# The six tiles for the weights' halves at six distances from a multiple of 512 bytes

## The chip, the cores and the metric

The kernel runs on one core of a Trainium2 chip. The metric is the device time of one execution in microseconds (us). The engines are named as in the profile: PE (TensorE matmul), PEld (its weight loads), DVE (VectorE), ACT (ScalarE), POOL (GpSimd), SP (SyncE, which issues DMAs).

## The reference

One layer of a diffusion transformer over 256 latent and 256 context tokens of width 2048, all in float32, batch 1, one layer deep. Cut to its core:

```python
mod = silu(c) @ w_mod + b_mod                      # six rows of 2048: sa, ca, ga, sm, cm, gm
h   = rmsnorm(x, w) * (1 + ca) + sa                # latent tokens; the context likewise with c_ctx
p   = h @ w_in                                     # q, k, v, pool input, two gates
a   = softmax(q1 k1) - lam * softmax(q2 k2)        # 8 heads, keys of latent and context
mix = (sig(g_a) * (rmsnorm(a v) @ w_a) + sig(g_b) * (pool(p) @ w_b)) @ w_o
x   = x + ga * mix
x   = x + gm * (relu(h2 @ w_ff1) ** 2 @ w_ff2)     # h2 = modulate(x), w_ff1 is 2048 x 8192
```

## The kernel before

Every weight is read from memory once, in chunks of 128 partitions x 1024 float32 (512 KB; the four `pool_w` chunks have 512). `load_next` brings a chunk into one of five `raw` tiles by a DMA on SP's queue and splits it: ACT rounds it to the matmul's reduced float32 (`act.copy(hi, raw)`, line 213) into a tile `whi`, and DVE subtracts (`vec.tensor_sub(lo, raw, hi)`, line 214) to get the rest, `wlo`. Activations are split into such pairs as well. A product is then three matmuls: high by high, low activation by high weight, high activation by low weight (`mm3`, lines 241 to 243; `xstat`, lines 410, 411 and 413; `ff1`, lines 939 and 942).

The order of the chunks is written out in a list by `plan`; `wchunk` hands out the next one and keeps two more loaded ahead. There are three `whi` and three `wlo` tiles (`bufs=3`). A new chunk takes any of the three whose last reader is done. Only the eight chunks of the first half of `w_k` go elsewhere, to a 16 KB tile `first` that holds four halves.

The tiles lie in SBUF in the order in which the code first asks for them, each row of a tile whole. So the three `whi` and three `wlo` tiles, each with a row of 4096 bytes, are neighbours. The ring of seven 16 KB tiles (`xT`, `cT`, `hL`, `hC`, `first`, later `act`, `mix` and others) lies ahead of them, and so do the nine 2 KB work tiles, the small ones, and the five `raw` tiles.

The work goes through stages. First the modulation stage: a loop over m = 1 to 7 multiplies chunks of `w_m` (`mod_chunk`, line 347), eight in a pass, into a row for four column blocks; `mod_rows` (line 352) copies it out, `mod_columns` turns it on PE, and `hidden` builds `hL` and `hC`, the modulated latent and context tokens. In the same loop `first_steps` works off, in steps of three matmuls, the first halves of `w_k` (latent `kx`, context `kc`) and `w_q`. The dictionary `carried` says after which chunk of a pass these begin, and after each `w_m` chunk one or two steps are taken:

```python
    for m in range(4, 8):
        carried[m] = ((0, "kc", m - 2), (2, "kx", m - 1), (4, "q", m - 1))
...
            gens += [first_steps(n, j) for at, n, j in carried[m] if at == i]
            todo = chain(*gens)
            steps(todo, 16 if i == 7 else 2 if i < 4 or m == 3 else 1)
```

So in a pass the `w_q` chunk comes after the fifth `w_m` chunk, and its four steps are taken one by one after the fifth, sixth, seventh and eighth. Then follow the rest of q, k and v, with the attention beside them, pooling, gates, `w_o`, and the feed-forward part in eight blocks (`ff1`, `ff2`). In these, chunks are used up one after the other.

The order of the instructions on each engine is not that of the code: a scheduler takes, for each engine, the earliest instruction in the code whose operands and tiles are ready by its own model of time, except where `tc.keep_in_program_order` (`pin`) holds an order. The order is then fixed in the program.

Of the kernel before, what the change touches and what calls it, by code (L numbers as in the profile page):

```python
# [11 lines left out]
F32 = mybir.dt.float32  # L12
F32R = mybir.dt.float32r
# [4 lines left out]
P = 128  # L18
# [30 lines left out]
def layer(ctx: ExitStack, tc, a, out):  # L49
    nc = tc.nc  # L50
    pool = ctx.enter_context(tc.tile_pool(name="sb", bufs=1))
# [23 lines left out]
    def s16(name, shape, dt=F32):  # L75
        return pool.tile(shape, dt, tag="s16", name=name, bufs=7)
# [34 lines left out]
    def raw_chunk(src, n=1024):  # L111
        raw = pool.tile([P, n], F32, tag="raw", name="raw", bufs=5)
        nc.sync.dma_start(raw, src)
        return raw
# [66 lines left out]
    def x1_tile():  # L181
        if not x1s:
            x1s.append(s16("x1", [P, 2, D]))
        return x1s[0]

    loaded = []
    done = [0]

    def load_next():
        key, rate = stream[len(loaded)]  # L190
        src = a[key[0]]
        for i in key[1:]:
            src = src[i]
        if key[0] == "prq":
            nc.sync.dma_start(prq, src)
            loaded.append((key, None, None))
            return
        if key[0] in ("cT", "x"):
            dst = cT[:, 4 * key[1]:4 * key[1] + 4, :] if key[0] == "cT" else x1_tile()[:, key[1], key[2] * 512:key[2] * 512 + 512]
            nc.sync.dma_start(dst, src)  # L200
            loaded.append((key, None, None))
            return
        n = src.shape[-1]
        raw = raw_chunk(src, n)
        if key[:2] == ("w_k", 0):
            if not first:
                first.append(s16("first", [P, 4, 1024], F32R))
            i = 2 * (key[2] % 2)
            hi, lo = first[0][:, i, :], first[0][:, i + 1, :]
        else:  # L210
            hi = pool.tile([P, n], F32R, tag="whi", name="whi", bufs=3)
            lo = pool.tile([P, n], F32R, tag="wlo", name="wlo", bufs=3)
        act.copy(hi, raw)  # L213
        vec.tensor_sub(lo, raw, hi.bitcast(F32))  # L214
        loaded.append((key, hi, lo))
        credit[0] += rate
        credit_rate[0] = rate
        while credit[0] >= 1.0:
            credit[0] -= 1.0
            if late[0] is not None:  # L220
                next(late[0], None)

    def wchunk(*key, ahead=AHEAD):
        while len(loaded) < min(done[0] + 1 + ahead, len(stream)) or loaded[done[0]][1] is None:
            if loaded and done[0] < len(loaded) and loaded[done[0]][1] is None:
                done[0] += 1
                continue
            load_next()
        got, hi, lo = loaded[done[0]]
        assert got == key, (got, key)  # L230
        loaded[done[0]] = None
        done[0] += 1
        tick()
        return hi, lo
# [857 lines left out]
```

## Time and profile before

| | |
|---|---|
| median of the runs shown | 1521.57 us (2 runs, 1521.33 to 1521.80) |
| the profiled execution | 1519.78 us, of which 1517.7 are the span from first to last instruction |
| granted TensorE clock | 0.994 |
| PE, DVE, ACT busy | 98%, 70%, 50% of the span |
| read from memory | 344.44 MB, 228 GB/s over the span |

In the profile a group of instructions is given by its line in the code, its engine and operation, the tiles written and read (without buffer numbers), shape and count. Behind the bar stand the group's busy time, the mean duration of one in ns, and the idle time of the engine ahead of them with what ended it. In the timeline the first column is the start in us, the second the duration (of a row with a count over 1: of them all). Durations of matmuls are those of a pipeline, and overlap: the distance of two starts is the pitch.

### The profile page before, as it was taken

What the parts mean: (1) busy time and instruction counts of PE and PEld (TensorE: products, weight loads), DVE (VectorE), ACT (ScalarE), POOL (GpSimd) and SP (SyncE); (2) the same over time, 40 slices, a digit from 0 to 9 for tenths busy, and PEclk for the clock granted to TensorE, in tenths of its full rate; (3) what the DMA queues carried; (4) which work ended last, traced back from release to release, by engine and by line L of the source; (5) the groups of instructions that cost most, each with busy time, mean ns of one, the idle gap of its engine ahead of it and who ended that gap; (6) DMA issues with size and microseconds to landing.
All of it is one profiled execution on the core that took longest, in us unless ns stands there. A gap on an engine that the chain in (4) does not pass through costs nothing.

```text
span 1517.7 us, 19767 instructions
## 1 busy us (share of the span) xinstructions
PE 1480.7 (98%) x7336; PEld 1232.8 (81%) x7336; DVE 1063.2 (70%) x1280; ACT 755.7 (50%) x1007; POOL 129.3 (9%) x124
## 2 busy tenths in 40 slices
PE   7899999999989999999999999999999999999998
PEld 5677877768878888888879988888888888888887
DVE  7799878777887767666757665666666555555675
ACT  6677534556655444444444554544444454444432
POOL 0100111000140000000000100100000000000170
PEclk9899999999999999999999999999999999999999
DMA  8888668556568787788755677767777666666664
GB/s 314 310 283 308 214 215 285 177 167 193 167 216 300 254 275 272 242 295 296 235 181 168 220 251 245 232 217 244 231 241 240 202 188 193 193 187 193 184 200 142
DMA packets 97439, 347.82 MB, mean 229 GB/s; under 512 B 11072, under 2 KB 11712, under 8 KB 97344
## 3 DMA queue, kind: packets, MB, share of 16 engines
q1 hardware_dynamic: 96768, 345.49, 70.4%
q8 instruction: 57, 0.93, 0.3%
q0 software_dynamic: 576, 1.08, 0.2%
q14 instruction: 38, 0.31, 0.1%
HBM read 344.44 MB, written 2.10 MB: 228 GB/s over the span
## 4 chain that ended last, share of the span: by engine, by line
PE 88%; issue 3%; DVE 3%; DMA 3%; ACT 1%; POOL 1%; DVEq 0%; SPq 0%; ACTq 0%; POOLq 0%
PE f L939 14%; PE f L411 8%; PE f L410 8%; PE f L413 8%; PE f L942 7%; PE pg L413 4%; PE pg L410 4%; PE pg L411 4%; PE pyy L410 2%; PE wo L410 2%; PE wo L413 2%; PE wo L411 2%; PE pyy L413 2%; PE pyy L411 2%; PE v L411 2%
## 5 line engine op out<-in xcount | busy, mean ns | idle before, releaser
L214 DVE TENSOR_TENSOR wlo<-raw,whi 128x1024 fp32r<-128x1024 f32 x507 | 628.6, 1244 | 365.2 <-ACT whi L213 350.9
L213 ACT CAST whi<-raw 128x1024 fp32r<-128x1024 f32 x507 | 529.8, 1047 | 587.3 <-PE f L411 178.1
L939 PE MATMUL f<-h,whi 128*128 128x512 f32 x896 | 224.2, 392 | 0.0
L411 PE MATMUL f<-whi,act 128*128 128x512 f32 x512 | 199.3, 389 | 0.0
L410 PE MATMUL f<-whi,act 128*128 128x512 f32 x512 | 199.3, 389 | 0.0
L939 PEld LDWEIGHTS f<-h,whi 128*128 128x128 f32 x896 | 161.5, 189 | 29.1
L588 DVE SCALAR_TENSOR_TENSOR macc<-raw,sil,macc 128x1024 f32<-128x1024 f32 x128 | 166.2, 1299 | 1.4 <-DMA raw<-in_w_cm_dram 0.8
L413 PE MATMUL f<-wlo,act 128*128 128x512 f32 x512 | 136.8, 389 | 0.0
L942 PEld LDWEIGHTS f<-h,wlo 128*128 128x128 f32 x896 | 122.2, 190 | 8.7
L942 PE MATMUL f<-h,wlo 128*128 128x256 f32 x896 | 124.9, 282 | 0.0
L413 PEld LDWEIGHTS f<-wlo,act 128*128 128x128 f32 x512 | 96.1, 188 | 20.0
L411 PEld LDWEIGHTS f<-whi,act 128*128 128x128 f32 x512 | 96.1, 188 | 19.8
L410 PEld LDWEIGHTS f<-whi,act 128*128 128x128 f32 x512 | 96.1, 188 | 19.8
L410 PE MATMUL pg<-whi,hL 128*128 128x512 f32 x256 | 100.5, 393 | 0.0
L411 PE MATMUL pg<-whi,hL 128*128 128x512 f32 x256 | 99.7, 389 | 0.0
L950 POOL TENSOR_TENSOR rsq<-relu 128x512 f32<-128x512 f32 x28 | 29.2, 1042 | 537.6 <-ACT relu L949 516.7
L413 PE MATMUL pg<-wlo,hL 128*128 128x512 f32 x256 | 68.6, 390 | 2.5 <-DVE wlo L214 2.5
L413 PEld LDWEIGHTS pg<-wlo,hL 128*128 128x128 f32 x256 | 48.0, 188 | 12.9 <-DVE wlo L214 2.9
L410 PEld LDWEIGHTS pg<-whi,hL 128*128 128x128 f32 x256 | 48.1, 188 | 10.1 <-issue 0.2
L411 PEld LDWEIGHTS pg<-whi,hL 128*128 128x128 f32 x256 | 48.1, 188 | 10.1 <-issue 0.2
L410 PE MATMUL wo<-whi,mix 128*128 128x512 f32 x128 | 49.9, 390 | 0.0
L411 PE MATMUL wo<-whi,mix 128*128 128x512 f32 x128 | 49.8, 389 | 0.0
(267 smaller groups left out, 2205.1 us busy)
## 6 DMA issues: line engine op xcount, KB each, us to landing
raw<-in_w_ff_dram SPq DMA_DIRECT2D x240, 512.0 KB, 4.3
raw<-in_w_m_dram SPq DMA_DIRECT2D x64, 512.0 KB, 4.9
raw<-in_w_ga_dram SPq DMA_DIRECT2D x32, 512.0 KB, 4.6
raw<-in_w_cm_dram SPq DMA_DIRECT2D x32, 512.0 KB, 4.6
raw<-in_w_gb_in_dram SPq DMA_DIRECT2D x32, 512.0 KB, 4.5
raw<-in_w_ga_in_dram SPq DMA_DIRECT2D x32, 512.0 KB, 4.4
raw<-in_w_sm_dram SPq DMA_DIRECT2D x32, 512.0 KB, 4.7
raw<-in_w_o_dram SPq DMA_DIRECT2D x32, 512.0 KB, 4.6
```

Of the source, the lines that this page charges most:

```text
L213: act.copy(hi, raw)
L214: vec.tensor_sub(lo, raw, hi.bitcast(F32))
L410: pe.matmul(banks[t], tok(h, k, 0, tt), wt, start=k == 0, stop=False)
L411: pe.matmul(banks[t], tok(h, k, 1, tt), wt, start=False, stop=False)
L413: pe.matmul(banks[t], tok(h, k, 0, tt), wt, start=False, stop=k == 2 * nk - 1)
L588: pin(vec.scalar_tensor_tensor(acc, raw, sil[:, 0, k:k + 1], acc, ALU.mult, ALU.add))
L939: pe.matmul(ps, hi[:, kk * P:kk * P + P], both(h2, k), start=k == 0, stop=False)
L942: pe.matmul(ps[:, T:2 * T], lo[:, kk * P:kk * P + P], act_slice(h2, k, 0), start=False, stop=k == KT - 1)
L950: gp.tensor_mul(sq, r, r)
```

## The change

The six tiles get names of their own, `whia` to `wloc`, each alone under its tag, and behind each a tile of 16 floats (64 bytes) is asked for that nothing uses. `half_tiles` makes them all at the first call; chunk number n then takes the pair n modulo 3.

```diff
+    halves = []
+    used = [0]
+
+    def half_tiles(n):
+
+        if not halves:
+            for part in ("whi", "wlo"):
+                for i in range(3):
+                    halves.append(pool.tile([P, 1024], F32R, tag=f"{part}{'abc'[i]}", name=f"{part}{'abc'[i]}", bufs=1))
+                    pool.tile([P, 16], F32, tag=f"gap{part}{'abc'[i]}", name="gap", bufs=1)
+        i = used[0] % 3
+        used[0] += 1
+        if used[0] <= 3:
+            return halves[i][:, 0:n], halves[3 + i][:, 0:n]
+        return [pool.tile([P, n], F32R, tag=f"{part}{'abc'[i]}", name=f"{part}{'abc'[i]}", bufs=1) for part in ("whi", "wlo")]
+
...
-            hi = pool.tile([P, n], F32R, tag="whi", name="whi", bufs=3)
-            lo = pool.tile([P, n], F32R, tag="wlo", name="wlo", bufs=3)
+            hi, lo = half_tiles(n)
```

## The prediction

> **What bounds the kernel now.** I read the page's busy shares and chain first, then the table by stage, then the costliest groups.
>
> ```profile
> PE 1480.7 (98%) x7336; PEld 1232.8 (81%) x7336; DVE 1063.2 (70%) x1280; ACT 755.7 (50%) x1007; POOL 129.3 (9%) x124
> PE 88%; issue 3%; DVE 3%; DMA 3%; ACT 1%; POOL 1%; DVEq 0%; SPq 0%; ACTq 0%; POOLq 0%
> 0.00:40.00 40.00, 28.36 (x132) 21.17 (x133) 28.62 (x45) 27.06 (x37) 1.82 (x6) 1.00 0.90 319
> 40.00:80.00 40.00, 35.72 (x135) 25.34 (x134) 32.99 (x48) 29.12 (x43) 7.23 (x4) 0.87 0.82 287
> 60.00:160.00 100.00, 97.45 (x428) 75.80 (x427) 90.45 (x149) 71.87 (x95) 0.00 (x0) 1.00 0.86 297
> 500.00:600.00 100.00, 100.00 (x450) 82.91 (x449) 70.75 (x68) 44.16 (x48) 1.48 (x2) 1.00 0.78 261
> 1000.00:1200.00 200.00, 200.00 (x1002) 170.19 (x1001) 130.31 (x135) 92.33 (x110) 8.34 (x8) 1.00 0.74 231
> ```
>
> The table's columns are the stretch, then busy time of PE, PEld, DVE, ACT and POOL, the granted clock, DMA share and GB/s. The reader is to see two regimes. From about 60 us on PE has no room: 97.45 of 100 us in the modulation stage, 100 of 100 later, at clock 1.00. In the first 60 us PE waits for weights: DMA share 0.90 in the first row, its highest. So the change can help only by shortening matmuls, and can hurt only where it leaves PE without work. DVE and ACT, which write the six tiles, have slack except in the modulation stage (90.45 and 71.87 of 100).
>
> **Part 1: the addresses.** Before, the six tiles are neighbours of 4096 bytes each, so all start at one distance from a multiple of 512. After, a 64-byte gap follows each: six distances. No instruction, byte or DMA is added by it, and `raw` is requested earlier and stays where it is. Do operands at one distance slow each other? The trace holds an experiment: for the first-half `w_k` chunks the halves go into `first`, in the ring of 16 KB tiles in which `hL` lies too. Adding up the code's row lengths from that ring to `whi` (single-value rows taken as 32 bytes) puts `whi` 256 bytes from it modulo 512. So these rows compare an output at `raw`'s distance with one 256 bytes off, and a matmul whose two operands lie at one distance with one whose operands lie 256 apart:
>
> ```profile
> L213 ACT CAST whi<-raw x507: 615/1053/1092, 11.5 to 1504.2; 128x1024 fp32r<-128x1024 f32 x168, 128x512 fp32r<-128x512 f32 x1
> L213 ACT CAST first<-raw x8: 1031/1053/1056, 27.1 to 153.4; 128x1024 fp32r<-128x1024 f32 x8
> L214 DVE TENSOR_TENSOR wlo<-raw,whi x507: 683/1225/2310, 12.5 to 1505.5; 128x1024 fp32r<-128x1024 f32 x168, 128x512 fp32r<-128x512 f32 x1
> L214 DVE TENSOR_TENSOR first<-raw,first x8: 1209/1225/1227, 28.8 to 154.5; 128x1024 fp32r<-128x1024 f32 x8
> L242 PE MATMUL w_k<-first,hL x32: 387/389/497, 30.1 to 165.1; 128*128 128x512 f32 x32
> L242 PE MATMUL w_q<-wlo,hL x32: 389/389/499, 36.2 to 167.8; 128*128 128x512 f32 x32
> ```
>
> The medians are equal to the nanosecond: 1053 and 1053, 1225 and 1225, 389 and 389. Steps of 64 bytes were not seen, so I bound them: zero from these pairs, and, from the other side, all of a matmul's pitch that does not grow with its length. The pitch is read in the feed-forward rows:
>
> ```profile
> 850.15 2.00 PE L939 MATMUL f<-h,whi 128*128 128x512 f32 x8
> 851.99 1.11 PE L942 MATMUL f<-h,wlo 128*128 128x256 f32 x8
> 852.95 0.86 PE L939 MATMUL f<-h,whi 128*128 128x512 f32 x3
> ```
>
> Eight of 512 columns take 851.99 - 850.15 = 1.84 us, 0.230 each; eight of 256 take 0.96 us, 0.120 each. Twice 0.120 less 0.230 is 0.010 us that does not grow with length; over 7336 matmuls that is 73 us. I take zero, as the pairs lie nearest; 73 us stays as a rival.
>
> [...]
>
> **Part 2: the rotation.** Before, a new chunk takes any of three `whi` (and `wlo`) tiles that is free. After, chunk n must take the tile of chunk n-3. Where chunks end in the order in which they began, these are the same. They do not in the modulation loop: `first_steps` spreads a `w_q` chunk's twelve matmuls over the next three `w_m` chunks. The third cast after the `w_q` cast then falls due while `w_q` is still being read. The timeline of loop passes 2, 6 and 7:
>
> ```profile
> 55.68 1.99 ACT L213 CAST whi<-raw 128x1024 fp32r<-128x1024 f32 x2
> 58.17 1.05 ACT L213 CAST whi<-raw 128x1024 fp32r<-128x1024 f32 x1 [0.50 <-PE mod L347]
> 61.34 1.05 ACT L213 CAST whi<-raw 128x1024 fp32r<-128x1024 f32 x1 [2.11 <-PE mod L347]
> 63.82 1.05 ACT L213 CAST whi<-raw 128x1024 fp32r<-128x1024 f32 x1 [1.44 <-PE mod L347]
> 67.70 0.39 PE L243 MATMUL w_q<-whi,hL 128*128 128x512 f32 x1
> ...
> 128.82 0.40 PE L241 MATMUL w_k<-first,hL 128*128 128x512 f32 x1
> 130.56 1.05 ACT L213 CAST whi<-raw 128x1024 fp32r<-128x1024 f32 x1 [0.63 <-DMA raw<-in_w_q_dram]
> 132.33 1.98 ACT L213 CAST whi<-raw 128x1024 fp32r<-128x1024 f32 x2
> 135.44 1.05 ACT L213 CAST whi<-raw 128x1024 fp32r<-128x1024 f32 x1 [1.13 <-DVE wlo L214]
> 137.86 0.61 PE L347 MATMUL mod<-whi,cv 128*128 128x512 f32 x2
> 138.31 0.62 PE L347 MATMUL mod<-wlo,cv 128*128 128x512 f32 x2
> 138.77 0.39 PE L241 MATMUL w_q<-whi,hL 128*128 128x512 f32 x1
> 139.22 0.39 PE L243 MATMUL w_q<-whi,hL 128*128 128x512 f32 x1
> 140.06 0.57 ACT L352 COPY rows<-mod 4x512 f32<-4x512 f32 x1
> 145.45 0.19 PEld L241 LDWEIGHTS w_k<-first,hL 128*128 128x128 f32 x1 [0.25 <-ACT hL L381]
> 152.24 1.05 ACT L213 CAST whi<-raw 128x1024 fp32r<-128x1024 f32 x1 [1.70 <-DVE wlo L214]
> 155.67 0.39 PE L243 MATMUL w_q<-whi,hL 128*128 128x512 f32 x1
> ```
>
> In pass 6 the `w_q` cast is at 130.56, two follow at 132.33, and the third, of the pass's last `w_m` chunk, starts at 135.44, while `w_q` is read until 139.22 + 0.39 = 139.61. Under the new rule it starts 4.17 us too early. In pass 2 (`w_q` is the second of the two at 55.68) it is 67.70 + 0.39 - 63.82 = 4.27, in pass 7 155.67 + 0.39 - 152.24 = 3.82. One such place stands in each of seven passes. In the first, before 60 us, PE waits for weights anyway: nothing. Six remain.
>
> What it costs in pass 6: the last `w_q` step (three matmuls, by these rows (139.22 - 138.77) / 2 = 0.225 each, 0.68 in all) must now go ahead of the last `w_m` chunk, at 137.86. Its third matmul then starts at 137.86 + 0.45 = 138.31 and ends at 138.70. Behind it come the cast, 1.05, the subtraction, 1.22, and the two `wlo` matmuls, 0.62: with no gap counted, to 141.59, where they now end at 138.31 + 0.62 = 138.93. The modulation row is late by about 2.7 us. Behind it wait `rows` (140.06), the turned columns, `hidden`, and the next pass's first `w_k` matmul on `hL`, which already starts last in that chain (0.25 us idle at 145.45). Behind the waiting cast stand, in ACT's queue, whatever casts are ordered after it; the kept `raw` buffer holds back one of SP's five.
>
> The cover: the next pass's `w_m` chunks write another bank and can go first. Each is four matmuls, 0.90 us; two of them cover 1.8 of 2.7. More would need weights that DMA, at share 0.86, has hardly brought yet. So about 0.9 us per place are left, 6 x 0.9 = 5.4 us. Without cover it is at most the whole overlap, 6 x 4.27 = 25.6; with full cover nothing. I take 5.4: PE's 2.55 idle us in 100 say that covers are mostly found, but the chain to 145.45 has no slack to give.
>
> After this stage chunks are used up in order, so the rotation is the old one; the 1.0 busy share of PE there hands any lost time to the end unchanged.
>
> **The sum.** Profiled execution 1519.78 us (span 1517.7 and 2.1 around it) plus 5.4 is 1525.2. The median of the runs shown is 1521.57, 1.8 above the profiled one, so the forecast is 1521.57 + 5.4, about 1527.
>
> **The rivals.**
> - *Nothing happens.* Addresses do not matter and the reordered matmuls cover each place: 1518 to 1525. For it: PE lists in this stage are already interleaved freely and full. Against: the chain that ends at 145.45 without slack.
> - *The loss feeds itself: slower.* A pass runs from one first `w_k` matmul to the next: 145.45 - 128.82 = 16.6 us. If nothing covers and the late `w_k` makes the next `w_q` late too, each of six passes grows by 2.7 to 4.27 us, say 3.5, and as long as a cast is late its `raw` stays held and SP cannot issue; at share 0.86 DMA cannot catch up, so as much again is lost: 6 x (3.5 + 3.5 x 0.86) = 39 us, 1561. It decides above 2% only from 30.4 / 6 = 5.1 us per place, more than any overlap alone.
> - *The operands do clash: faster.* Then the fixed 10 ns of pitch go, in part or whole: up to 73 us, 1449. For it: only that 64-byte steps were not seen. Against: the three equal pairs. A spread that does only half its work gives 1485.
>
> **Chances.** Forecast case, 3 to 26 us lost: 0.60. Nothing happens: 0.29. Loss feeds itself: 0.06, of which 0.05 beyond 2%. Clash gone: 0.05, of which 0.03 beyond 2%. The range, 1517 to 1547, is the first two cases with their bounds, 0.89 of the chance by these numbers. Faster by over 2% (under 1491) 0.03, within 2% 0.92, slower (over 1552) 0.05; 2% is about what a measurement of this kernel can tell from no change.
>
> **What would show it.** Step 1: casts of 1053, subtractions of 1225 and matmul pitches of 0.225 to 0.230 us at 512 columns stay for all six tiles alike; a pitch that differs by tile proves it wrong. Step 2: in passes 2 to 7 the last `w_q` matmul stands ahead of the pass's last `w_m` matmuls, the cast waits for PE `w_q`, and PE's idle time in 60 to 170 us grows by some 5 us; from the `w_v` stage on the two traces run parallel. I am wrong if the order of work after that stage differs too, or if PE's time there changes.

## The result and the profile after

The median after is 1545.34 us (2 runs, 1544.12 to 1546.55) against 1521.57 before: a ratio of 1.0156, 95% interval 1.0113 to 1.0200. The change costs about 24 us. The forecast was 1527, so the time lies inside the range, near its upper end. That is luck: the upper part of the range was made for a rotation that nothing covers, and what filled it was the addresses. The step that was priced at 5.4 us cost about 9, and the step that was priced at nothing cost 12 to 16.

The kernel is as bound by PE as it was: its share is 97% where it was 98%, but the same 7336 matmuls are busy for 1501.1 us, 20.4 more than the 1480.7 of before. That row and the chain of work that ended last, from the page of the kernel after:

```profile
PE 1501.1 (97%) x7336; PEld 1230.4 (80%) x7336; DVE 1062.7 (69%) x1280; ACT 753.7 (49%) x1007; POOL 128.6 (8%) x124
PE 88%; DVE 4%; ACT 3%; DMA 2%; issue 2%; POOL 1%; SPq 0%; DVEq 0%; ACTq 0%; POOLq 0%
```

The table by stage of the kernel after (stretch, busy time of PE, PEld, DVE, ACT, POOL, granted clock, DMA share, GB/s) says where:

```profile
60.00:160.00 100.00, 92.34 (x383) 68.11 (x382) 83.74 (x142) 66.19 (x89) 0.00 (x0) 0.98 0.83 277
500.00:600.00 100.00, 100.00 (x441) 81.25 (x441) 70.20 (x68) 42.91 (x47) 1.46 (x2) 1.00 0.78 258
1000.00:1200.00 200.00, 200.00 (x997) 168.00 (x996) 131.22 (x137) 93.80 (x113) 10.86 (x11) 1.00 0.73 234
```

There are two losses of different kinds. In the modulation stage PE has gaps: busy 92.34 of 100 us where it was 97.45. From 500 to 600 us PE has none in either kernel, at clock 1.00, and yet 441 matmuls fit where 450 did. The busy share of 1.0 hides this; the count shows it. By the starts of the same matmuls in both traces, the first gate matmul comes 8.0 us later (430.0 to 438.0), the first of `w_o` 15.3 later (704.1 to 719.4), and the end 24.0 later (1517.7 to 1541.7): about 8 us in the modulation stage, 16 spread behind it.

**The first loss** is the predicted one. The timelines of ACT and PE of the kernel after, in the pass where `w_q` sits in `whib`, and the row that groups these waits from 28 to 180 us:

```profile
146.69 1.05 ACT L228 CAST whib<-raw 128x1024 fp32r<-128x1024 f32 x1 [3.73 <-PE w_q L258]
```

```profile
146.26 0.39 PE L258 MATMUL w_q<-whib,hL 128*128 128x512 f32 x1
146.49 0.62 PE L362 MATMUL mod<-whic,cv 128*128 128x512 f32 x2
...
147.87 0.64 PE L362 MATMUL mod<-whib,cv 128*128 128x512 f32 x2
...
149.05 0.73 PE L362 MATMUL mod<-wlob,cv 128*128 128x512 f32 x2
```

```profile
ACT whib L228 <- PE w_q L258: 6.8, 3, 3.7
```

The cast of the third chunk behind `w_q` stands idle 3.73 us until the last `w_q` matmul (146.26) has read `whib`; only then can `whib` be written and the pass's last `mod` pair (147.87, 149.05) run. Of the 6.8 us in the last row, 2.31 lie in the first pass, at 40 us, where before has such a wait too (1.53 us). The third wait of the row, 0.76 us, is in the pass ahead of this one. So of the six places that the prediction counted, two show a clear wait of ACT for `w_q`; in the others the last `w_q` matmul is done, or nearly so, when the cast falls due.

**The second loss** is in the pitch, the distance of two starts. Timelines of PE in the second feed-forward product, before, then after:

```profile
914.82 0.39 PE L410 MATMUL f<-whi,act 128*128 128x512 f32 x1
915.05 0.39 PE L411 MATMUL f<-whi,act 128*128 128x512 f32 x1
915.27 0.39 PE L410 MATMUL f<-whi,act 128*128 128x512 f32 x1
915.50 0.39 PE L411 MATMUL f<-whi,act 128*128 128x512 f32 x1
915.73 1.07 PE L413 MATMUL f<-wlo,act 128*128 128x512 f32 x4
916.63 0.39 PE L410 MATMUL f<-whi,act 128*128 128x512 f32 x1
```

```profile
920.27 0.39 PE L425 MATMUL f<-whic,act 128*128 128x512 f32 x1
...
922.13 1.10 PE L428 MATMUL f<-wloc,act 128*128 128x512 f32 x4
923.07 0.40 PE L425 MATMUL f<-whia,act 128*128 128x512 f32 x1
```

Before, eight matmuls take 916.63 - 914.82 = 1.81 us, 0.226 each. After, the twelve of one chunk take 923.07 - 920.27 = 2.80 us, 0.233 each. Over the whole trace the mean pitch of such matmuls (lines 410, 411 and 413 of before), by the distances of their starts, was 226.7 to 226.9 ns; after it is 229 to 234, by tile. The duration column (0.39, 0.40) does not show this: the profile models the ends of matmuls, and only starts are to be trusted. There are 3744 of these matmuls, about 4.9 ns more each: 18 us. The 112 chunks of `w_ff1`, where the half is loaded as weights, give a little back: a chunk's sixteen matmuls take 2785 ns in the mean where they took 2792.

Casts and subtractions have not changed. All instructions of the two lines on one tile each, after (the three figures are shortest, median and longest in ns):

```profile
L228 ACT CAST whia<-raw x170: 617/1052/1082, 10.9 to 1528.0; 128x1024 fp32r<-128x1024 f32 x169, 128x512 fp32r<-128x512 f32 x1
L229 DVE TENSOR_TENSOR wloa<-raw,whia x170: 684/1225/2316, 12.0 to 1529.3; 128x1024 fp32r<-128x1024 f32 x169, 128x512 fp32r<-128x512 f32 x1
```

### The profile page after: what moved, and what is told of

The parts are those of the page before. It is cut to its first block, busy times and chain, and to the rows that moved or that the text cites. A ratio compares the mean times of both kernels' runs of the same rounds, so it can differ in the third digit from the quotient of the medians.

```text
span 1541.7 us, 19770 instructions
## 1 busy us (share of the span) xinstructions
PE 1501.1 (97%) x7336; PEld 1230.4 (80%) x7336; DVE 1062.7 (69%) x1280; ACT 753.7 (49%) x1007; POOL 128.6 (8%) x124
## 4 chain that ended last, share of the span: by engine, by line
PE 88%; DVE 4%; ACT 3%; DMA 2%; issue 2%; POOL 1%; SPq 0%; DVEq 0%; ACTq 0%; POOLq 0%
PE f L954 13%; PE f L428 8%; PE f L425 8%; PE f L426 8%; PE f L957 7%; PE pg L428 4%; PE pg L425 4%; PE pg L426 4%; PE pyy L428 2%; PE v L428 2%; PE wo L428 2%; PE pyy L425 2%; PE wo L425 2%; PE v L426 2%; PE wo L426 2%; PE pyy L426 2%
## 5 line engine op out<-in xcount | busy, mean ns | idle before, releaser
L229 DVE TENSOR_TENSOR wloc<-raw,whic 128x1024 fp32r<-128x1024 f32 (+1 forms) x169 | 210.0, 1243 | 132.8 <-ACT whic L228 126.7
L229 DVE TENSOR_TENSOR wloa<-raw,whia 128x1024 fp32r<-128x1024 f32 x170 | 212.1, 1248 | 127.3 <-ACT whia L228 122.6
L229 DVE TENSOR_TENSOR wlob<-raw,whib 128x1024 fp32r<-128x1024 f32 x168 | 208.4, 1240 | 127.2 <-ACT whib L228 121.2
L228 ACT CAST whic<-raw 128x1024 fp32r<-128x1024 f32 (+1 forms) x169 | 176.1, 1042 | 208.5 <-PE f L426 62.1
L228 ACT CAST whia<-raw 128x1024 fp32r<-128x1024 f32 x170 | 178.0, 1047 | 200.8 <-PE f L426 62.5
L228 ACT CAST whib<-raw 128x1024 fp32r<-128x1024 f32 x168 | 175.5, 1045 | 204.1 <-PE f L426 60.9
L954 PE MATMUL f<-h,whib 128*128 128x512 f32 x304 | 76.9, 395 | 0.0
L425 PE MATMUL f<-whic,act 128*128 128x512 f32 x172 | 68.0, 395 | 0.0
L425 PE MATMUL f<-whia,act 128*128 128x512 f32 x172 | 67.8, 394 | 0.0
L426 PE MATMUL f<-whic,act 128*128 128x512 f32 x172 | 67.7, 393 | 0.0
L426 PE MATMUL f<-whia,act 128*128 128x512 f32 x172 | 67.5, 393 | 0.0
L426 PE MATMUL f<-whib,act 128*128 128x512 f32 x168 | 65.8, 392 | 0.0
L425 PE MATMUL f<-whib,act 128*128 128x512 f32 x168 | 65.8, 391 | 0.0
```

What stands on the lines that cost most here:

```text
L425: pe.matmul(banks[t], tok(h, k, 0, tt), wt, start=k == 0, stop=False)
L426: pe.matmul(banks[t], tok(h, k, 1, tt), wt, start=False, stop=False)
L954: pe.matmul(ps, hi[:, kk * P:kk * P + P], both(h2, k), start=k == 0, stop=False)
```

## The experiments

**A coordinate.** Added up from the code's row lengths, the ring of 16 KB tiles, where the activations lie, stands at 224 modulo 512 bytes in each row. Before, the six half tiles all stand at 480: 256 away, so 0 modulo 256. After, they are 0, 64, 128 (`whia`, `whib`, `whic`) and 192, 0, 64 (`wloa`, `wlob`, `wloc`) away modulo 256. "Distance" below is this figure. `rotation_only` has the order of PE's matmuls of after, all others have that of before.

### Which of the two parts

`rotation_only`: after without its gaps.

```diff
-                    pool.tile([P, 16], F32, tag=f"gap{part}{'abc'[i]}", name="gap", bufs=1)
```

> The changed kernel without the six 64-byte gaps: six tiles alone under their tags, fixed rotation, all at one distance as before. In the changed kernel the third matmul stage begins 8 us late (first gate matmul 438.0 against 430.0 us) and 16 us more are lost behind that. Theory 1 (two causes that add): the rotation costs the 8 us of the modulation stage and nothing behind it: 1530, PE pitch 0.2267 us in the feed-forward part. Theory 2 (all is the rotation, later losses included): 1545.

`gaps_only`: before, with the same 64 bytes behind each half tile, any free tile taken.

```diff
-            hi = pool.tile([P, n], F32R, tag="whi", name="whi", bufs=3)
-            lo = pool.tile([P, n], F32R, tag="wlo", name="wlo", bufs=3)
+            hi = pool.tile([P, 1040], F32R, tag="whi", name="whi", bufs=3)[:, 0:n]
+            lo = pool.tile([P, 1040], F32R, tag="wlo", name="wlo", bufs=3)[:, 0:n]
```

> The kernel before with rows of 1040 floats of which 1024 are used: the six tiles lie where they lie in the changed kernel, but any free tile is taken and the order of instructions on every engine is that of before. Theory 1: only the slower matmul pitch is left, 16 us: 1537, pitch by tile 0.229 to 0.234 us. Theory 2: 1521.6, pitch 0.2267.

Measured: `rotation_only` 1530.85 against 1520.69, ratio 1.0059 (1.0039 to 1.0078), some 9 us by the ratio; `gaps_only` 1534.22, ratio 1.0081 (1.0061 to 1.0102), some 12 us (by the medians 10.2 and 13.5). The tables by stage, `rotation_only` and then `gaps_only`:

```profile
60.00:160.00 100.00, 92.60 (x385) 68.64 (x384) 84.24 (x141) 65.96 (x89) 0.00 (x0) 0.98 0.83 280
500.00:600.00 100.00, 100.00 (x451) 82.90 (x450) 70.75 (x69) 44.15 (x48) 1.47 (x2) 1.00 0.80 264
```

```profile
60.00:160.00 100.00, 95.88 (x423) 75.22 (x422) 89.14 (x146) 70.80 (x95) 0.00 (x0) 1.00 0.88 293
500.00:600.00 100.00, 100.00 (x443) 81.54 (x442) 70.55 (x68) 42.32 (x46) 1.46 (x2) 1.00 0.78 259
```

The two losses come apart cleanly. Rotation alone has the gaps in the modulation stage (92.60) and 451 matmuls from 500 to 600 us, 450 before; the distances alone have nearly no gaps there (95.88) and 443 matmuls. Added, 0.59% and 0.81% make 1.40%, inside the interval of the 1.56%.

### Is it the fixed order or the six names

`names_free_order`: `rotation_only`, but each chunk is given the tile that before gave it, from a written list; later chunks go round by three, as before did.

```diff
-        i = used[0] % 3
+            i = int(order[c]) if c < len(order) else int(order[len(order) - 3 + (c - len(order)) % 3])
```

> The kernel with the fixed rotation and no gaps, but each chunk is given, out of the six named tiles, the one that the kernel before gave it (the tile that a w_q chunk still holds is passed over). The order on PE is then that of the kernel before. Theory 1 (the fixed rotation makes a w_m chunk wait for w_q's last reader): 1521, the time of before. Rival (six tags with one buffer each cost by themselves): 1530 as with the rotation.

Measured: 1520.40 against 1520.35, ratio 1.0005 (0.9995 to 1.0015). The modulation stage in its table:

```profile
60.00:160.00 100.00, 97.01 (x426) 75.33 (x425) 90.17 (x151) 71.75 (x95) 0.00 (x0) 1.00 0.86 298
```

PE is back at 97.01. Six tiles under six names cost nothing; what costs the 9 us is that chunk n must take the tile of chunk n-3.

### What about the addresses

In `gaps_only` several things change together: the tiles' distances from each other, from the activations, from `raw`, and from any fixed boundary. `halves_192` keeps the six as close neighbours and moves all of them, and what comes behind them, by 192 bytes; `all_192` gives the six the same addresses, but moves everything else with them.

```diff
 # halves_192
+            if not gap:
+                gap.append(pool.tile([P, 48], F32, tag="gap", name="gap"))
             hi = pool.tile([P, n], F32R, tag="whi", name="whi", bufs=3)
 # all_192, ahead of the first tile
+    pool.tile([P, 48], F32, tag="gap", name="gap")
```

> The kernel before with one gap of 192 bytes ahead of the six tiles, which stay at one distance among themselves; nothing else moves. Theory A (the distance of what PE streams from what it loads as weights decides, modulo 512): they now stand to the 16 KB tiles as wloa did in the changed kernel, whose pitch was 0.2335 against 0.2267: 3744 matmuls of lines 410 to 413 by 6.8 ns are 25 us, 1547. Theory B (only a change of distance from one tile to the next costs): 1521.6, pitch 0.2267. Theory C (ACT and DVE, writing one of the six at another distance while PE reads another): 1521.6.

> The kernel before with one gap of 192 bytes ahead of all tiles: the six have the very addresses of the run with the gap ahead of them alone, and the 16 KB tiles have moved with them. Theories A, B and C: 1521.6, pitch 0.2267. Theory D (the address itself decides, not the distance to the other operand): the same time as with the gap ahead of the six alone, 1547 if that is slow.

Measured: `halves_192` 1539.24, ratio 1.0119 (1.0104 to 1.0134), streamed pitch 233.3 to 233.4 ns in all three lines; `all_192` 1520.77, ratio 1.0001 (0.9990 to 1.0012), pitch 226.7 to 226.9. Timeline of PE in `halves_192`:

```profile
915.08 1.10 PE L416 MATMUL f<-wlo,act 128*128 128x512 f32 x4
916.02 0.40 PE L413 MATMUL f<-whi,act 128*128 128x512 f32 x1
916.25 0.39 PE L414 MATMUL f<-whi,act 128*128 128x512 f32 x1
916.48 0.40 PE L413 MATMUL f<-whi,act 128*128 128x512 f32 x1
916.72 0.39 PE L414 MATMUL f<-whi,act 128*128 128x512 f32 x1
```

From 916.02 to 916.48 two matmuls take 0.46 us; the starts come 236 and 231 ns apart by turns. So the slow pitch needs no spread among the six: all at one distance of 192 have it, 233.3 to 233.4 ns. And it does not hang on absolute addresses: the same addresses with the rest moved along have the old pitch, 226.7 to 226.9. What counted in these two runs is where the halves lie against something ahead of them. That `halves_192` was forecast slower than it came out has a part in `w_ff1`, where a half is not streamed but loaded as weights, and the activation streams past it: there its pitch fell, at 512 columns from 229.9 to 229.0 ns and at 256 from 119.1 to 115.7. At 34 ns for each of 112 chunks that is 3.8 of the missing 8 us.

### Against whom: PE's own reads, or what ACT, DVE and the DMAs do

`ff2_held_192` is `halves_192` with the chunks of `w_ff2` left out: no DMA, cast or subtraction for them; the second feed-forward product reads the last three pairs over and over. It computes something else there, with the same matmuls.

```diff
+        if key[0] == "w_ff2":
+            loaded.append((key,) + recent[len(loaded) % 3])
...
+            return
...
+        recent[:] = (recent + [(hi, lo)])[-3:]
```

> The kernel with the 192-byte gap ahead of the six, in which w_ff2 is left out: no DMA, cast or subtraction for its chunks; the matmuls of ff2 read the three pairs of tiles that ff1 loaded last. Theory A (PE's own two reads, the streamed half and the weight load of the activations): the pitch in ff2 stays at 236 and 231 ns by turns, mean 0.2335 us, though ACT and DVE write nothing there. Theory C (ACT, DVE or DMA writes meet PE's reads): it falls to 0.2267.

The single run took 1538.77 us. Table row and timeline of PE in a stretch of the second product, and the table row of `halves_192` for the same stretch behind them:

```profile
1090.00:1130.00 40.00, 40.00 (x173) 32.25 (x172) 11.28 (x13) 2.10 (x2) 0.00 (x0) 1.00 0.22 66
1100.00 0.39 PE L424 MATMUL f<-whi,act 128*128 128x512 f32 x1
1100.23 0.40 PE L425 MATMUL f<-whi,act 128*128 128x512 f32 x1
1100.47 0.39 PE L424 MATMUL f<-whi,act 128*128 128x512 f32 x1
...
1101.87 0.39 PE L427 MATMUL f<-wlo,act 128*128 128x512 f32 x1
```

```profile
1090.00:1130.00 40.00, 40.00 (x174) 32.20 (x173) 27.09 (x27) 15.82 (x16) 1.04 (x1) 1.00 0.70 233
```

ACT falls from 15.82 to 2.10 us of 40, DVE from 27.09 to 11.28, the DMA share from 0.70 to 0.22, and PE does no more for it: 173 matmuls against 174, and eight of them in 1101.87 - 1100.00 = 1.87 us, 0.234 each, in the same pattern of 231 and 236. So the extra time does not come from what was taken away of the other engines' work and of the DMAs. That it lies between PE's own two operands, the streamed half and the activation that is loaded as weights, is inferred: they are what is left that the 192 bytes touch, and how the two meet no run shows.

### The map, and its period

The same gap tile with 64, 16 and 32 floats ahead of `whi` (`halves_256`, `halves_64`, `halves_128`), and with 64 floats between `whi` and `wlo` (`lo_256`).

> The kernel before with one gap of 256 bytes ahead of the six: distance 0 from the 16 KB tiles modulo 512 where it was 256. Theory A with a good distance at 0 as well (the w_k chunks in first and the wlob tile of the changed kernel settled at 226 to 227 ns): pitch 0.2267 in lines 410 to 413, 1521. If only 256 is good: 0.230 or more, 1535 or more.

> The kernel before with one gap of 256 bytes between the whi and the wlo tiles: distances 256 and 0. Theory A (each distance is good by itself, and passing from one to the other costs nothing): 1521, or 1 to 2 us less where ff1's line 942 runs faster at distance 0 (117 against 119 ns in the changed kernel's wlob). Theory B (a change of distance costs): pitch over 0.228 after each change, 1530 or more.

> The kernel before with one gap of 64 bytes ahead of the six: distance 64 from the 16 KB tiles, modulo 256. Theory A with a period of 256: the pitch is not 0.2267 in lines 410 to 413; from the changed kernel, whose whib and wloc tiles stood at 64 and alternated between 226 and 237 ns, 0.229 to 0.233: 9 to 24 us, 1529 to 1544.

> The kernel before with one gap of 128 bytes ahead of the six: distance 128, modulo 256. If the period is 256: slow as whic in the changed kernel, 0.232, 20 us, 1540. If the period is 128: pitch 0.2267, 1520.

Measured, with the pitches as means of distances of starts in ns (streamed: lines 410, 411 and 413 of before; `w_ff1`: one chunk's eight of 512 and eight of 256 columns):

| kernel | distance modulo 256 | ratio (95% interval) | streamed | `w_ff1` chunk |
|---|---|---|---|---|
| before | 0 | 1 | 226.7 | 2792 |
| `halves_256` | 0 | 1.0000 (0.9990 to 1.0009) | 226.7 | 2792 |
| `lo_256` | 0 | 1.0000 (0.9990 to 1.0011) | 226.7 | 2792 |
| `halves_64` | 64 | 1.0024 (1.0015 to 1.0033) | 228.9 | 2774 |
| `halves_128` | 128 | 1.0138 (1.0121 to 1.0155) | 232.5 | 2810 |
| `halves_192` | 192 | 1.0119 (1.0104 to 1.0134) | 233.4 | 2758 |

From 500 to 600 us the matmuls that fit number, in the order of the table, 450, 450, 450, 447, 440 and 438. In these moves the pitch repeats at 256 bytes: moving all six by 256 gives back the old one (226.7 ns), moving them by 128 does not (232.5). `lo_256`, from which a gain of 1 to 2 us was hoped for, gave nothing, and lost nothing: with changes between tiles 256 and 0 away the pitch was 226.7 ns and the ratio 1.0000. `halves_64` lost less than expected: its streamed pitch lies at the low end of the 229 to 233 that was forecast, and `w_ff1` gained 18 ns a chunk, 2 us. Which distance came out best depends on which operand streams: of the four, 0 for a streamed half (226.7 ns), and 192 for a chunk of `w_ff1` (2758 ns), whose halves are loaded as weights. There it differs by length as well: the matmuls of 512 columns took 229.0 ns at 192 in `halves_192` and 232.9 at 64 (`whib` in the kernel after), those of 256 columns 115.7 at 192 in `halves_192` and 114.0 at 64 (`wloc` in the kernel after).

### A version that uses the map

`two_places`: `names_free_order` with each half tile longer than its chunk, so that a half can stand at one of two offsets: distance 0 where it is streamed, 192 in the first feed-forward product. The small tiles go from 12 to 8 buffers for room.

```diff
+                    SPOT[part, i] = (1072, 0, 48) if at % 2 == 0 else (1040, 16, 0)
...
+            row, x, f = SPOT[part, i]
...
+            o = x if streamed else f
+            out.append(t[:, o:o + n])
...
+            hi, lo = half_tiles(n, key[0] not in ("w_ff1", "w_ff1a"))
```

> The order of tiles of the kernel before, with each half at one of two places in its longer row: distance 0 from the 16 KB tiles, modulo 256, where it is streamed, and 192 in w_ff1 and w_ff1a, where it is the weight load and the activations are streamed (the small tiles are eight instead of twelve, for room). In the run with the 192-byte gap, eight matmuls of ff1's first line and eight of its second took 8 x 229.0 + 8 x 115.7 = 2758 ns against 8 x 229.9 + 8 x 119.1 = 2792 before. Theory A: 112 such groups by 34 ns are 3.9 us less, 1516 where before is 1520 (ratio 0.9975), and lines 410 to 413 stay at 0.2267. If only the mean over all matmuls counts and not the distance in each: 1520 or more.

Measured: 1515.94 (11 runs) against 1520.36, ratio 0.9979 (0.9970 to 0.9988): 3.2 us less by the ratio, 4.4 by the medians, where 3.9 were expected. That is less than both kernels. PE's row of its page, and its table:

```profile
PE 1477.3 (98%) x7336; PEld 1230.0 (81%) x7336; DVE 1063.6 (70%) x1280; ACT 755.8 (50%) x1007; POOL 129.3 (9%) x124
```

```profile
500.00:600.00 100.00, 100.00 (x451) 82.89 (x450) 70.75 (x68) 44.13 (x48) 1.47 (x2) 1.00 0.79 261
1000.00:1200.00 200.00, 200.00 (x1007) 170.19 (x1006) 130.29 (x135) 92.45 (x109) 8.33 (x8) 1.00 0.72 232
```

Where halves are streamed (500 to 600 us) it is as before, 451 matmuls; from 1000 to 1200 us, where the two feed-forward products take turns, 1007 matmuls fit where 1002 did. PE is busy for 3.4 us less than before. The starts say where: a chunk of `w_ff1` takes 2756 ns where it took 2792, which is 4.0 us over 112 chunks, and the streamed pitch is 226.7 to 226.8 ns, as before. The order of PE's matmuls is that of before too.

## Why the prediction was right and wrong

**What bounds the kernel** held: PE without room from 60 us on hands every loss to the end. "So the change can help only by shortening matmuls, and can hurt only where it leaves PE without work" did not: matmuls can also get longer, and that was the larger loss.

**Part 1** failed at "I take zero, as the pairs lie nearest". The pairs were true, but they compare a distance of 0 with one of 256, which the map shows to be one and the same place. And they compare matmul durations (389 and 389), which the profile models and which are still 0.39 to 0.40 in kernels that are 6 ns slower per matmul; the pitch of starts was the row to read. "Steps of 64 bytes were not seen" was the right doubt, but the bound made of it had one sign only: the fixed 10 ns could go, so "the operands do clash: faster". A bound on the slow side was missing. Before stood at the best of the four places measured for its streamed halves (226.7 ns, against 228.9 to 233.4), and each of the others lost there. The term was 0 and measured some 12 us by `gaps_only`. That casts and subtractions would stay at 1053 and 1225 was right (1052 and 1225 after).

**Part 2** had the right mechanism, stage and sign. The cast waits for PE `w_q`, the last `w_q` matmul stands ahead of the pass's last `mod` matmuls, and PE's idle time from 60 to 170 us grew in `rotation_only` from 2.55 to 8.03 us, by 5.5 where "some 5 us" was expected. That it comes in six equal parts did not hold: the largest, 3.00 us from 68 to 76, lies where no cast waits for `w_q`: there PE waits for a cast (0.74 us) and a subtraction (1.18 us) into `whib` and `wlob`. The term was mis-sized, 5.4 against 9.0 (6 to 12 by the interval). A part that the sum lacked is seen in the table of `rotation_only` in steps of 4 us:

```profile
68.00:72.00 4.00, 2.78 (x10) 1.27 (x8) 3.97 (x7) 2.89 (x5) 0.00 (x0) 1.00 0.83 255
72.00:76.00 4.00, 2.22 (x11) 1.60 (x12) 2.92 (x5) 2.38 (x6) 0.00 (x0) 1.00 0.98 356
...
132.00:136.00 4.00, 3.83 (x17) 2.82 (x15) 3.48 (x7) 2.45 (x5) 0.00 (x0) 1.00 0.91 290
136.00:140.00 4.00, 2.67 (x8) 1.61 (x9) 3.68 (x9) 2.93 (x5) 0.00 (x0) 0.90 0.97 374
140.00:144.00 4.00, 4.00 (x14) 3.16 (x13) 3.52 (x6) 2.51 (x3) 0.00 (x0) 0.67 0.73 239
144.00:148.00 4.00, 4.00 (x19) 3.29 (x18) 1.22 (x1) 0.92 (x1) 0.00 (x0) 1.00 0.64 216
```

Behind a step in which PE is idle for a third of the time, the granted clock is 0.90 and then 0.67, and 14 matmuls run where 19 do at clock 1.00; an estimate from the two clocks is 0.10 x 4 + 0.33 x 4 = 1.7 us more. The clock of `names_free_order` is 1.00 over all of 60 to 160 us. That the idle time brings the lower clock is not shown: behind the longer one, from 68 to 76 us, the clock stays at 1.00. Idle time and clock make 5.5 + 1.7 = 7.2 us, and by the starts of the same matmuls `rotation_only` is 6.9 us behind before at the first gate matmul (436.9 against 430.0). Behind that its profiled execution loses 3.8 us more, in steps near 447 and 800 us; `names_free_order` loses 3.9 us in the same places, so they do not belong to the rotation. That the six places feed each other into 39 us was refuted.

**"From the `w_v` stage on the two traces run parallel"** is the sentence that the profile refutes first: the distance grows from 8.0 us at the gates to 24.0 at the end. The text had named this as its own test ("a pitch that differs by tile proves it wrong"), and by tile it does: 229.1 for `whib` and 233.8 for `wloa` in the streamed matmuls.

**What stays open.** Why the pitch at a distance of 192 goes 236, 231 by turns was not settled, and no run shows it. Nor does one show why `whia` is slower in after than at the same distance in before: behind tiles at other distances it has a mean of 231 ns, and only from the ninth matmul in a row on, which few runs of matmuls reach, 226 to 228; in `lo_256`, where the distances that change are equal modulo 256, the mean stays at 226.7. The period rests on two moves by 256 bytes and on steps of 64; finer steps were not run.

## What to carry to other kernels

When PE has no idle time, count the matmuls in a stretch and measure the distance of their starts; busy shares and durations hid a pitch that was 3% worse here. Choose the distance modulo 256 bytes between a streamed operand and the one loaded as weights, which here was worth 226.7 against 233.4 ns, and measure again after each edit that adds or resizes a tile, since 64 bytes ahead of the halves moved them all here (228.9 ns in `halves_64`). Buffers that are taken in turn cost nothing here where they were given back in turn (451 matmuls from 500 to 600 us in `rotation_only`, 450 before); where one was held longer than the others, taking the tiles that were free, as before did, brought the time back (1520.40 in `names_free_order`, 1530.85 in `rotation_only`).

## What the runs showed of the hardware

With the instructions of before and only the addresses changed, moving the streamed operand against the loaded one made the pitch of a 512-column matmul 226.7, 228.9, 232.5 or 233.4 ns at 0, 64, 128 or 192 bytes modulo 256. At 192, with ACT busy 2.10 us of 40 where it was 15.82 and the DMA share 0.22 where it was 0.70, eight such matmuls still took 1.87 us, 0.234 each. With the roles turned round the order of the places is another: 2758 ns for a chunk of `w_ff1` at 192, 2774 at 64, 2792 at 0, 2810 at 128. One idle stretch of PE in the modulation stage of `rotation_only` (2.67 us busy of 4, clock 0.90) was followed by 4 us at a granted clock of 0.67, in which 14 matmuls ran where 19 do at 1.00; a longer one (5.00 us busy of 8) was followed by a clock of 1.00, so when this happens is open.
